# Opening of a hybrid streaming encoder step: token tiles multiplied by norm_pre into buffers of their own

## The chip, the cores and the metric

The kernel runs on one core of a Trainium2 chip. The metric is the device time of one execution in microseconds, and of several executions the median. Times inside an execution come from the hardware profiler; they are counted from the start of the profiled span.

## The reference

One inference step of a one-layer encoder. Its input is 1024 prompt frames of one new stream and 16 frames of each of 8 running streams (128 sample rows in all), 2048 wide, all in float32.

```python
def rms_norm(x, g):
    xf = x.astype(jnp.float32)
    y = xf * lax.rsqrt(jnp.mean(xf * xf, axis=-1, keepdims=True) + EPS)
    return (y * g.astype(jnp.float32)).astype(x.dtype)
...
h = rms_norm(xp, norm_pre[l])
q_sb, k_sb, v_sb, gate_sb, q_r, k_r, v_r, gate_r = project(h, w_in[l], pos_p)
```

`project` is one product with `w_in` (2048 x 8192), whose columns are the queries, keys, values and gates of eight stick-breaking heads and of eight retention heads. Stick-breaking attention over the past keys, chunked retention, a normalisation per head, a gate, an output product with `w_out` and a second normalisation follow; then `x` is added. The sample rows go through the same with cached keys, values and states. What the change touches is only the first line: `h = x * rstd * norm_pre`, row by row.

## The kernel before

The tokens are nine tiles of 128 rows: eight of the prompt and one of the sample rows. Two groups are projected one after the other. Group 0 has prompt tiles 0 to 3 and the sample tile; group 1 has prompt tiles 4 to 7. A projection needs the normalised tokens transposed, with the 2048 features on the partitions, and keeps them in on-chip memory as two arrays: a high part `mh` (ScalarE writes the value rounded to float32r) and a low part `ml` (VectorE subtracts the high part from the value). The helper `split` (lines 129 and 130) makes both, for tokens and for weights (`wh`, `wl`). A float32 product is then three products: wh by mh, wh by ml, wl by mh, in this order (line 227), for each of 16 blocks of features.

The opening, the first 45 us or so, works on the five tiles of group 0. They are called first to fifth here: prompt tiles 0, 1, 2, 3 and the sample tile. For each of them:

- SP's queue loads the tile (`load_x`, line 356, 1 MB, four buffers `xt`). The gain vector `norm_pre` comes broadcast to all partitions as `gpre` in two loads of half the columns, behind the first tile's load (line 380). Further loads on the same queue are four blocks of weights `wr` for the first projection (line 213), the constants, and then the weights of the next projections.
- `stats` takes the mean square: ScalarE squares the tile and sums (line 362, out to `sq`, sum in `ssq`), VectorE computes mean plus epsilon `p0v` (line 137), ScalarE takes the root (line 138), and VectorE does a reciprocal and four small steps of refinement (lines 139 to 143), which end in `p0r`, the reciprocal root.
- For the first four tiles VectorE builds `dg`, a diagonal matrix with `p0r` on it (line 389). For the fifth it multiplies the whole tile by `p0r` in place (line 396).
- The tile is multiplied by `gpre` in place, in eight pieces of 256 columns (line 392). `PRE_POOL` lists the tiles that GpSimd multiplies: second, third and fourth. VectorE multiplies the first and the fifth. As it is in place, a piece can only be written once ScalarE has squared the tile.
- `turn` transposes it on TensorE: four quarters of four 128x128 blocks each, against `dg` (line 372), which scales by the reciprocal root at the same time, or against the identity for the fifth tile (line 370). The profile shows two matmul rows for each block. The results lie in four PSUM buffers `p0t`, one for each quarter, which the `split` of that quarter empties into `mh` and `ml`.

After the second tile TensorE does the first 48 products of the first projection, for the 256 tokens that are there (accumulator of 256 columns); the products for the other 384 tokens come after the fifth tile. After these the projections run one after the other, while a job (`stage_rest`) normalises and stores the tiles of group 1 in between, and the attention, retention and output stages follow.

A scheduler orders the instructions of each engine from the program's text and its own estimates; each engine then runs its list strictly in that order, and waits on semaphores for what it reads, and for buffers that it overwrites. The order on an engine can thus change where the text is changed only nearby. SP, ScalarE and GpSimd also issue transfers from their lists; SP carries the loads of the opening.

Of the kernel before, what the change touches and what calls it, by code (L numbers as in the profile page):

```python
# [9 lines left out]
F32 = mybir.dt.float32  # L10
F32R = mybir.dt.float32r
AF = mybir.ActivationFunctionType
ALU = mybir.AluOpType
# [3 lines left out]
P = 128  # L17
D = 2048
# [6 lines left out]
NT = PT + 1  # L25
SAMPLE = PT
WQ = 4
PRE_POOL = (1, 2, 3)
PRE_DIAG = (0, 1, 2, 3)
PRE_CUT = 8  # L30
PRE_G = 2
# [27 lines left out]
def tile_hybrid_step(  # L59
# [26 lines left out]
    nc = tc.nc  # L86
# [12 lines left out]
    def x_rows(t):  # L99
        return x_prompt[0, t * P : (t + 1) * P, :] if t < PT else xs_flat  # L100
# [27 lines left out]
    def split(hi, lo, src):  # L128
        nc.scalar.activation(hi, src, AF.Copy)  # L129
        nc.vector.tensor_tensor(lo, src, hi.bitcast(F32), ALU.subtract)  # L130

    def inv_rms(pool, ssq, n, name):
        shape = list(ssq.shape)
        v = pool.tile(shape, F32, name=f"{name}v")
        r = pool.tile(shape, F32, name=f"{name}r")
        u = pool.tile(shape, F32, name=f"{name}u")
        nc.vector.tensor_scalar(v, ssq, 1.0 / n, EPS, ALU.mult, ALU.add)
        nc.scalar.activation(r, v, AF.Sqrt)
        nc.vector.reciprocal(r, r)
        nc.vector.tensor_tensor(u, r, r, ALU.mult)  # L140
        nc.vector.tensor_tensor(u, u, v, ALU.mult)
        nc.vector.tensor_scalar(u, u, -0.5, 1.5, ALU.mult, ALU.add)
        nc.vector.tensor_tensor(r, r, u, ALU.mult)
        return r
# [41 lines left out]
    def drain(job):  # L186
        while job is not None and not job.done:
            tick()
# [20 lines left out]
    def load_w(col):  # L209
        hs, ls = [], []  # L210
        for w in range(KT // WQ):
            wr = wp.tile([P, WQ, P], F32, name="wr", tag="wr")
            nc.sync.dma_start(
                wr,
                w_in[0, w * WQ * P : (w + 1) * WQ * P, col : col + P].rearrange("(k p) e -> p k e", p=P),
            )
            wh = wp.tile([P, WQ, P], F32R, name="wh", tag="wh")
            wl = wp.tile([P, WQ, P], F32R, name="wl", tag="wl")
            split(wh, wl, wr)
            yield w, wh, wl  # L220

    def products(mov, acc, pieces, w, wh, wl):
        hi, lo = mov
        for j in range(WQ):
            for n, (lhs, rhs) in enumerate(((wh, hi), (wh, lo), (wl, hi))):
                for a, (o, m) in zip(acc, pieces):
                    last = nc.tensor.matmul(  # L227
                        a[:, :m],
                        lhs[:, j, :],
                        rhs[w][:, j, o : o + m],  # L230
                        start=(w == 0 and j == 0 and n == 0),
                        stop=(w == KT // WQ - 1 and j == WQ - 1 and n == 2),
                    )
                anchor[0] = last
                tick()
        return last

    def acc_banks(g):
        return [accp.tile([P, 512], F32, name=f"acc{i}", tag=f"acc{i}") for i in range(len(g["pieces"]))]
# [60 lines left out]
    with ExitStack() as s1:  # L300
# [39 lines left out]
        def load_rope(gi):  # L340
            n = GROUPS[gi]["n"]
            ropes[:] = [tp.tile([P, n], F32, name=c, tag=c) for c in ("cosT", "sinT")]
            nc.sync.dma_start(ropes[0], c_cos[gi][:, :n])
            nc.sync.dma_start(ropes[1], c_sin[gi][:, :n])
# [3 lines left out]
        with tc.tile_pool(name="p0", bufs=2) as p0, tc.tile_pool(name="p0s", bufs=1) as p0s, tc.tile_pool(  # L348
            name="p0p", bufs=4, space=PSUM
        ) as p0p:  # L350
            warm = p0s.tile([P, 1], F32, name="warm")
            nc.scalar.activation(warm, eps, AF.Sqrt)

            def load_x(t):
                xt = p0.tile([P, D], F32, name="xt", tag="xt", bufs=4)
                nc.sync.dma_start(xt, x_rows(t))
                return xt

            def mean_square(xt):
                ssq = p0.tile([P, 1], F32, name="ssq", tag="ssq")  # L360
                sq = p0s.tile([P, D], F32, name="sq0", tag="sq0")
                nc.scalar.activation(sq, xt, AF.Square, accum_out=ssq)
                return inv_rms(p0, ssq, D, "p0")

            def turn(q, xt, scale=None):
                pt = p0p.tile([P, 4, P], F32, name="p0t", tag="p0t")
                for j in range(4):
                    blk = xt[:, (4 * q + j) * P : (4 * q + j + 1) * P]
                    if scale is None:
                        nc.tensor.transpose(pt[:, j, :], blk, ident)  # L370
                    else:
                        nc.tensor.matmul(pt[:, j, :], blk, scale, start=True, stop=True)
                return pt

            tiles = g0["tiles"]
            loaded = [load_x(tiles[0])]
            gpre = p0s.tile([P, D], F32, name="gpre")
            for c in range(PRE_G):
                cs = slice(c * D // PRE_G, (c + 1) * D // PRE_G)
                nc.sync.dma_start(gpre[:, cs], norm_pre[0, cs].partition_broadcast(P))  # L380
            loaded += [load_x(t) for t in tiles[1:3]]

            def stats(i):
                xt = loaded[i]
                rstd = mean_square(xt)
                dg = None
                if i in PRE_DIAG:
                    dg = p0.tile([P, P], F32, name="dg", tag="dg")
                    nc.vector.tensor_scalar(dg, ident, rstd, None, ALU.mult)
                for c in range(PRE_CUT):  # L390
                    cs = slice(c * D // PRE_CUT, (c + 1) * D // PRE_CUT)
                    (nc.gpsimd if i in PRE_POOL else nc.vector).tensor_tensor(
                        xt[:, cs], xt[:, cs], gpre[:, cs], ALU.mult
                    )
                if dg is None:
                    nc.vector.tensor_scalar(xt, xt, rstd, None, ALU.mult)
                return dg

            scales = [stats(0)]
            for i, t in enumerate(tiles):  # L400
                if i + 1 < len(tiles):
                    scales.append(stats(i + 1))
                cs = slice(i * P, (i + 1) * P)
                for q in range(KT // 4):
                    pt = turn(q, loaded[i], scales[i])
                    split(mov[0][q][:, :, cs], mov[1][q][:, :, cs], pt)
                if i == 1:
                    w4 = list(load_w(col(4, 0)))
                    loaded += [load_x(t) for t in tiles[3:]]
                    acc = acc_banks(g0)  # L410
                    for w in w4:
                        products(mov, acc[:1], g0["pieces"][:1], *w)
            for w in w4:
                last = products(mov, acc[1:], g0["pieces"][1:], *w)

            nc.sync.dma_start(dec, c_dec)
            load_rope(0)
            with nc.allow_non_contiguous_dma(reason="small gains"):
                nc.sync.dma_start(gains[:, 0, :], sb_gain[0].rearrange("(h p) -> p h", p=P))
                nc.sync.dma_start(gains[:, 1, :], ret_gain[0].rearrange("(h p) -> p h", p=P))  # L420

            def stage_rest():
                for i, t in enumerate(GROUPS[1]["tiles"]):
                    hs = p0s.tile([P, KT, P], F32, name="hs", tag="hs")
                    xt = load_x(t)
                    yield 6

                    rstd = mean_square(xt)
                    nc.vector.scalar_tensor_tensor(xt, xt, rstd, gpre, ALU.mult, ALU.mult)
                    yield 12  # L430
                    for q in range(KT // 4):
                        with tc.issue_after(last.ins) if q == 0 else nullcontext():
                            pt = turn(q, xt)
                        nc.scalar.activation(hs[:, 4 * q : 4 * q + 4, :], pt, AF.Copy)
                        yield 3
                    nc.scalar.dma_start(s_h[:, :, i * P : (i + 1) * P], hs)

            job = Job(stage_rest(), D_REST)
            first = ret_inputs(g0, mov, 0, list(zip(acc, g0["pieces"])))
            ret_values(g0, mov, 0)  # L440
            first = *first[:2], pair["r"][:, :, 0, :], dict(rg=gate(project(g0, mov, col(7, 0)), "rg"))
            drain(job)
# [765 lines left out]
```

## Time and profile before

| | us |
|---|---|
| median of 3 runs | 2405.88 |
| lowest and highest | 2405.13, 2412.4 |
| span of the profiled execution, first to last instruction | 2398.4 |
| TensorE busy in the span | 2331.4 (97%) |
| VectorE, ScalarE, GpSimd busy | 1257.5, 919.6, 643.0 |

The profile gives the span of its execution and no other time for it. In the profile PE is TensorE (PEld its weight load), DVE is VectorE, ACT is ScalarE, POOL is GpSimd and SP the engine that issues most transfers. A row of a time line has the start and the length in us, the engine, the line of the kernel, the operation, the tile written and the tiles read, shapes and a count; in brackets stands how long the engine was idle before and what it waited for. Rows with a count over 1 are merged, and instructions of one engine overlap a little in their rows. A row of DMA issues ends with the size in KB and the time from issue to landing.

### The profile page before, as it was taken

To read this page: it belongs to the slowest core of one execution; us is meant where nothing else is said; L and a number is where in the kernel's file an instruction comes from. 1 tells how busy PE (TensorE), PEld (TensorE's weight loads), DVE (VectorE), ACT (ScalarE), POOL (GpSimd) and SP (SyncE) were. 2 spreads that over 40 slices of the span, in tenths; PEclk is the share of its full clock that TensorE was granted. 3 is DMA by queue.
4 is the path that set the end of the run, shared out by engine and by line. 5 is a ranking of instruction groups with operands and counts; after the bars stand their busy time and mean duration, and the time that the engine had idled before them with its cause. 6 is when DMAs were issued, how large, how long until landed. Compare 5 with 4: busy or idle time off the path is not lost.

```text
span 2398.4 us, 40493 instructions
## 1 busy us (share of the span) xinstructions
PE 2331.4 (97%) x14832; PEld 2093.7 (87%) x14832; DVE 1257.5 (52%) x2434; ACT 919.6 (38%) x1933; POOL 643.0 (27%) x1029
## 2 busy tenths in 40 slices
PE   7999999999999999998999999999999999999998
PEld 7998899999999999988878889889898887878787
DVE  7245545445554555445545554554554665564544
ACT  6323333333333333324433434343343454543343
POOL 3144353444344353443202112020221230000000
PEclk9999999999999999999999999999999999999999
DMA  7658879797889879798975565565565666765554
GB/s 244 164 131 209 162 169 196 169 203 166 184 179 194 184 167 194 176 198 198 200 191 151 139 157 149 133 157 146 142 160 139 157 177 181 231 207 176 191 182 132
DMA packets 674890, 418.68 MB, mean 175 GB/s; under 512 B 224513, under 2 KB 619777, under 8 KB 672257
## 3 DMA queue, kind: packets, MB, share of 16 engines
q1 hardware_dynamic: 524272, 285.99, 47.8%
q0 software_dynamic: 32256, 71.36, 13.6%
q10 hardware_dynamic: 118160, 58.74, 9.1%
q8 instruction: 116, 1.90, 0.4%
q14 instruction: 86, 0.70, 0.1%
HBM read 336.24 MB, written 79.69 MB: 173 GB/s over the span
## 4 chain that ended last, share of the span: by engine, by line
PE 87%; DVE 4%; DMA 4%; issue 2%; ACT 1%; POOL 1%; ACTq 0%; DVEq 0%; SPq 0%; POOLq 0%
PE acc L227 45%; PE accn L286 17%; PE a L1029 5%; PE a L1030 5%; PE a L1028 5%; PE pa L616 3%; PE z L586 2%; DMA wr<-w_in 1%; PE zc L659 1%; PE pd L726 1%; DMA mr<-s_h 1%; DVE wl L130 1%; PE pa L770 1%; DVE out L1090 1%; PE rs L752 1%
## 5 line engine op out<-in xcount | busy, mean ns | idle before, releaser
L227 PE MATMUL acc<-mh,wh 128*128 128x256 f32 (+2 forms) x2304 | 664.3, 341 | 6.4 <-ACT wh L129 6.0
L227 PE MATMUL acc<-ml,wh 128*128 128x384 f32 (+2 forms) x2304 | 663.0, 340 | 0.0
L130 DVE TENSOR_TENSOR wl<-wr,wh 128x512 fp32r<-128x512 f32 (+1 forms) x576 | 392.7, 688 | 515.5 <-ACT wh L129 508.3
L227 PE MATMUL acc<-mh,wl 128*128 128x256 f32 (+2 forms) x2304 | 658.9, 339 | 0.6 <-DVE wl L130 0.5
L129 ACT ACTIVATE wh<-wr 128x512 fp32r<-128x512 f32 (+1 forms) x576 | 356.9, 624 | 713.1 <-PE acc L227 243.4
L227 PEld LDWEIGHTS acc<-mh,wh 128*128 128x128 f32 x2304 | 420.2, 189 | 43.3 <-ACT wh L129 7.1
L227 PEld LDWEIGHTS acc<-mh,wl 128*128 128x128 f32 x2304 | 424.4, 189 | 31.4 <-issue 2.1
L227 PEld LDWEIGHTS acc<-ml,wh 128*128 128x128 f32 x2304 | 422.6, 189 | 33.2 <-issue 5.3
L643 POOL DMA_DIRECT2D kc<-cache_sb_k x512 | 332.4, 655 | 369.8 <-DVE kcT L681 207.5
L286 PE MATMUL accn<-whn,mh 128*128 128x256 f32 x1152 | 329.0, 287 | 0.9 <-ACT whn L129 0.8
L286 PE MATMUL accn<-wln,mh 128*128 128x256 f32 x1152 | 326.2, 283 | 0.7 <-DVE wln L130 0.7
L286 PE MATMUL accn<-whn,ml 128*128 128x256 f32 x1152 | 326.0, 283 | 0.0
L286 PEld LDWEIGHTS accn<-whn,mh 128*128 128x128 f32 x1152 | 220.5, 192 | 10.8 <-issue 6.7
L1029 PE MATMUL a<-wl,mh 128*128 128x512 f32 (+1 forms) x576 | 219.7, 381 | 7.8 <-DVE wl L130 7.8
L286 PEld LDWEIGHTS accn<-wln,mh 128*128 128x128 f32 x1152 | 221.2, 192 | 1.7 <-DVE wln L130 0.9
L286 PEld LDWEIGHTS accn<-whn,ml 128*128 128x128 f32 x1152 | 221.2, 192 | 0.0
L1030 PE MATMUL a<-wh,ml 128*128 128x512 f32 (+1 forms) x576 | 218.9, 380 | 0.0
L1028 PE MATMUL a<-wh,mh 128*128 128x512 f32 (+1 forms) x576 | 218.0, 380 | 0.0
L130 DVE TENSOR_TENSOR wln<-wrn,whn 128x512 fp32r<-128x512 f32 x128 | 87.5, 687 | 119.2 <-ACT whn L129 118.5
L129 ACT ACTIVATE whn<-wrn 128x512 fp32r<-128x512 f32 x128 | 80.1, 633 | 152.2 <-PE accn L286 69.8
L1029 PEld LDWEIGHTS a<-wl,mh 128*128 128x128 f32 x576 | 108.3, 188 | 30.5 <-DVE wl L130 9.9
L479 POOL DMA_DIRECT2D be<-s_be x128 | 94.2, 742 | 132.7 <-DMA s_be<-be 114.7
(189 smaller groups left out, 2604.8 us busy)
## 6 DMA issues: line engine op xcount, KB each, us to landing
wr<-w_in SPq DMA_DIRECT2D x384, 256.0 KB, 4.2
wr<-w_out SPq DMA_DIRECT2D x184, 256.0 KB, 3.6
wrn<-w_in SPq DMA_DIRECT2D x128, 256.0 KB, 3.1
kc<-cache_sb_k POOLq DMA_DIRECT2D x512, 64.0 KB, 4.5
vc<-cache_sb_v SPq DMA_DIRECT2D x64, 512.0 KB, 8.6
xt<-x_prompt SPq DMA_DIRECT2D x8, 1024.0 KB, 5.6
xr<-x_prompt SPq DMA_DIRECT2D x8, 1024.0 KB, 6.2
out<-out ACTq DMA_DIRECT2D x12, 512.0 KB, 2.9
```

What stands on the lines that cost most here:

```text
L129: nc.scalar.activation(hi, src, AF.Copy)
L130: nc.vector.tensor_tensor(lo, src, hi.bitcast(F32), ALU.subtract)
L227: last = nc.tensor.matmul(a[:, :m], lhs[:, j, :], rhs[w][:, j, o : o + m], start=(w == 0 and j == 0 and n == 0), stop=(w == KT // WQ - 1 a ...
L286: anchor[0] = nc.tensor.matmul(a, lhs[q][:, jj, ts], rhs[:, j, :], start=(w == 0 and j == 0 and n == 0 and t % 2 == 0), stop=(w == KT // 2 ...
L479: q.dma_start(raw[32 * i : 32 * i + 32, :].rearrange("p (k a) -> p k a", a=32), s[:, :, 32 * i : 32 * i + 32].rearrange("k (j b) a -> b (k ...
L586: nc.tensor.matmul(z[:, :c], q2[a][:, i * P : (i + 1) * P], k2[b][:, s : s + c], start=(m == 0), stop=(m == 2),)
L616: nc.tensor.matmul(po[:, :P], at[:, j, :], vn[:, j, :], start=(j == 0), stop=(j == t))
L643: nc.gpsimd.dma_start(kc[32 * i : 32 * i + 32, :].rearrange("p (k d) -> p k d", d=32), cache_k[0, 2 * c + j, s * 512 : (s + 1) * 512, h, 3 ...
L659: mm = nc.tensor.matmul(z[r, :], qp[:, j, r], ready[2 * j + c // 2][:, c % 2, :], start=(j == 0), stop=(j == 1),)
L1028: nc.tensor.matmul(a[:, :width], hi[q][:, j, ts], wh, start=(k == 0), stop=False)
L1029: nc.tensor.matmul(a[:, :width], hi[q][:, j, ts], wl, start=False, stop=False)
L1030: nc.tensor.matmul(a[:, :width], lo[q][:, j, ts], wh, start=False, stop=(k == KT - 1))
```

## The change

Each of the five tiles is now multiplied by `gpre` into a buffer of its own, `xg` (two buffers), and no longer in place; the turns read `xg`. The multiplication moves from `stats` into a new function `gain`, which is called ahead of `stats`, so it stands in the text ahead of the square. `PRE_POOL` now lists pairs of a tile and the parity of a piece: of the second and of the fifth tile GpSimd multiplies the odd pieces and VectorE the even ones; the third and fourth tile stay with GpSimd, the first with VectorE. The fifth tile's scaling works on `xg`.

```diff
-PRE_POOL = (1, 2, 3)
+PRE_POOL = ((1, 1), (2, 0), (2, 1), (3, 0), (3, 1), (4, 1))
...
                 if i in PRE_DIAG:
                     dg = p0.tile([P, P], F32, name="dg", tag="dg")
                     nc.vector.tensor_scalar(dg, ident, rstd, None, ALU.mult)
-                for c in range(PRE_CUT):
-                    cs = slice(c * D // PRE_CUT, (c + 1) * D // PRE_CUT)
-                    (nc.gpsimd if i in PRE_POOL else nc.vector).tensor_tensor(
-                        xt[:, cs], xt[:, cs], gpre[:, cs], ALU.mult
-                    )
                 if dg is None:
-                    nc.vector.tensor_scalar(xt, xt, rstd, None, ALU.mult)
+                    nc.vector.tensor_scalar(gained[i], gained[i], rstd, None, ALU.mult)
                 return dg

+            gained = {}
+
+            def gain(i):
+                xt = loaded[i]
+                xg = gained[i] = p0.tile([P, D], F32, name="xg", tag="xg", bufs=2)
+                for c in range(PRE_CUT):
+                    cs = slice(c * D // PRE_CUT, (c + 1) * D // PRE_CUT)
+                    pool = (i, c % 2) in PRE_POOL
+                    (nc.gpsimd if pool else nc.vector).tensor_tensor(xg[:, cs], xt[:, cs], gpre[:, cs], ALU.mult)
+
+            gain(0)
             scales = [stats(0)]
             for i, t in enumerate(tiles):
                 if i + 1 < len(tiles):
+                    gain(i + 1)
                     scales.append(stats(i + 1))
                 cs = slice(i * P, (i + 1) * P)
                 for q in range(KT // 4):
-                    pt = turn(q, loaded[i], scales[i])
+                    pt = turn(q, gained[i], scales[i])
                     split(mov[0][q][:, :, cs], mov[1][q][:, :, cs], pt)
```

More of the change, by code (lines that the diff above doesn't have):

```diff
@@ L389, in stats @@
                     nc.vector.tensor_scalar(dg, ident, rstd, None, ALU.mult)
+                if dg is None:
+                    nc.vector.tensor_scalar(gained[i], gained[i], rstd, None, ALU.mult)
+                return dg
+            gained = {}
+            def gain(i):
+                xt = loaded[i]
+                xg = gained[i] = p0.tile([P, D], F32, name="xg", tag="xg", bufs=2)
                 for c in range(PRE_CUT):
                     cs = slice(c * D // PRE_CUT, (c + 1) * D // PRE_CUT)
-                    (nc.gpsimd if i in PRE_POOL else nc.vector).tensor_tensor(
-                        xt[:, cs], xt[:, cs], gpre[:, cs], ALU.mult
-                    )
-                if dg is None:
-                    nc.vector.tensor_scalar(xt, xt, rstd, None, ALU.mult)
-                return dg
+                    pool = (i, c % 2) in PRE_POOL
+                    (nc.gpsimd if pool else nc.vector).tensor_tensor(xg[:, cs], xt[:, cs], gpre[:, cs], ALU.mult)
+            gain(0)
             scales = [stats(0)]
```

## The prediction

> **What bounds the kernel now.** I began with busy shares and slices on the page, then the stretches of the opening, then the chain and the time lines.
>
> ```profile
> PE 2331.4 (97%) x14832; PEld 2093.7 (87%) x14832; DVE 1257.5 (52%) x2434; ACT 919.6 (38%) x1933; POOL 643.0 (27%) x1029
> PE  7999999999999999998999999999999999999998
> ```
> ```profile
> 0.00:45.00 45.00, 29.30 (x202) 28.22 (x203) 32.16 (x81) 28.93 (x46) 19.18 (x30) 0.96 0.84 275
> 45.00:60.00 15.00, 15.00 (x98) 14.98 (x97) 13.91 (x37) 9.88 (x19) 0.00 (x0) 1.00 0.44 150
> 60.00:190.00 130.00, 129.98 (x1008) 127.00 (x1007) 49.21 (x100) 43.87 (x89) 40.98 (x66) 1.00 0.60 154
> ```
> The columns of a stretch are its length, the busy time of TensorE, its weight load, VectorE, ScalarE and GpSimd, the granted clock, the DMA share and GB/s. TensorE is the bound: 97% busy, and gapless from 45 to 190 us (15.00 of 15.00, then 129.98 of 130.00). Only the first slice is weak: of the first 45 us TensorE works 29.30. The change lies wholly there, so its worth is one number: when the unbroken run of products starts. The chain gives the start of that run, the time line of TensorE what comes before it:
>
> ```profile
> 43.46 16.01 PE acc L227 x99
> ```
> ```profile
> 10.63 6.71 PE L372 MATMUL p0t<-dg,xt 128*128 128x128 f32 x32 [10.63 <-DVE dg L389]
> 19.52 5.44 PE L372 MATMUL p0t<-dg,xt 128*128 128x128 f32 x32 [2.19 <-DVE p0v L137]
> 24.72 0.36 PE L227 MATMUL acc<-mh,wh 128*128 128x256 f32 x1
> 25.04 0.28 PE L227 MATMUL acc<-mh,wl 128*128 128x256 f32 x1
> 30.55 3.73 PE L372 MATMUL p0t<-dg,xt 128*128 128x128 f32 x32
> 35.67 3.81 PE L372 MATMUL p0t<-dg,xt 128*128 128x128 f32 x32 [1.38 <-issue]
> 40.43 0.63 PE L370 MATMUL p0t<-ident,xt 128*128 128x128 f32 x4 [0.95 <-DVE xt L396]
> 43.40 0.44 PE L227 MATMUL acc<-ml,wh 128*128 128x384 f32 x1
> ```
> TensorE turns five token tiles (I call them first to fifth): from 10.63, 19.52, 30.55, 35.67 and 40.43, with the first 48 products (128x256) between the second and third. From 43.40 it never stops. The second tile started late:
>
> ```profile
> 11.57 1.91 ACT L362 ACTIVATE sq<-xt 128x2048 f32<-128x2048 f32 x1 [3.32 <-DMA xt<-x_prompt]
> 13.65 11.95 POOL L392 TENSOR_TENSOR xt<-xt,gpre 128x256 f32<-128x256 f32 x16 [12.27 <-ACT sq L362]
> ```
> GpSimd multiplies the second tile only after its square, eight pieces of 11.95/16 = 0.75 us from 13.65 to 19.6.
>
> **The change, part by part.** Counts do not change: 24 multiplies on GpSimd, 16 on VectorE, the same loads. The built programs have the same order on TensorE, GpSimd and SP; only about a hundred instructions of VectorE and ScalarE are reordered.
>
> *First tile.* Now all eight multiplies stand ahead of the reciprocal, four even ahead of the mean (p0v). They need the gain vector, which comes in two loads:
>
> ```profile
> 1.26 0.89 SPq L380 DMA_DIRECT2D gpre<-norm_pre  x2
> gpre<-norm_pre SPq DMA_DIRECT2D x1, 512.0 KB, 6.5
> 1.73 0.42 SPq L380 DMA_DIRECT2D gpre<-norm_pre  x1
> gpre<-norm_pre SPq DMA_DIRECT2D x1, 512.0 KB, 7.2
> 7.86 0.15 DVE L137 TENSOR_SCALAR p0v<-ssq 128x1 f32<-128x1 f32 x1 [6.36 <-ACT sq L362]
> 10.30 0.28 DVE L389 TENSOR_SCALAR dg<-ident,p0r 128x128 f32<-128x128 f32 x1
> 10.49 0.75 DVE L392 TENSOR_TENSOR xt<-xt,gpre 128x256 f32<-128x256 f32 x2
> 28.55 0.17 DVE L139 RECIPROCAL p0r<-p0r 128x1 f32<-128x1 f32 x1 [0.27 <-ACT p0r L138]
> 28.74 0.16 DVE L140 TENSOR_TENSOR p0u<-p0r 128x1 f32<-128x1 f32 x1
> ```
> The halves land at 7.8 and 8.9. Two multiplies in a row take 0.75, so each adds 0.34. Four run from 7.8 to 9.15, p0v then stands at 9.15 instead of 7.86, four more run to 10.55, and only then come the reciprocal and four dependent small steps at 0.19 each: dg at 11.5, done 11.8. Before, those steps were hidden between the multiplies. TensorE starts at 11.85, **1.2 us later**. If the gain vector came a microsecond earlier, 0.2 of it would remain.
>
> *Second tile.* Four pieces each on GpSimd and VectorE, from the landing at 11.5 and without the square. Both engines then read two tiles at once:
>
> ```profile
> 30.97 1.77 DVE L392 TENSOR_TENSOR xt<-xt,gpre 128x256 f32<-128x256 f32 x2
> 45.89 0.63 ACT L129 ACTIVATE wh<-wr 128x512 fp32r<-128x512 f32 x1
> 16.65 1.90 ACT L362 ACTIVATE sq<-xt 128x2048 f32<-128x2048 f32 x1
> 16.60:20.05 3.45, 1.26 (x11) 1.10 (x11) 3.11 (x8) 3.22 (x6) 3.45 (x6) 1.00 1.05 399
> 20.05:23.46 3.41, 3.41 (x19) 3.41 (x18) 2.38 (x5) 1.81 (x5) 3.41 (x5) 0.51 0.98 379
> ```
> Beside GpSimd a piece took 1.77/2 = 0.88 instead of 0.34; four from 11.7 end at 15.2. That is early enough, since the diagonal comes later: it now follows two low parts of the first tile, whose second quarter is turned at 11.85 + 16 x 0.21 + 0.4 = 15.6 (6.71/32 = 0.21 a turn), split by 17.0, and three small steps and dg bring 17.8. The first tile's turns end at 11.85 + 6.7 = 18.5. So the second tile starts at 18.4, 1.1 earlier, without the 2.2 us pause. That pause preceded a stretch at a granted clock of 0.51. Without it I take the 3.73 of the third tile for its 32 turns: end at **22.1** instead of 24.7. Its bounds are 3.73 and 6.7 (the first tile's cold rate). ScalarE is the next limit: the third tile's square (1.90) now precedes the third and fourth high parts of the first tile, which end near 19.2; with 0.6 for each high part of a tile or a weight, the second tile's last high part ends near 22.9. The two new buffers make GpSimd's third tile wait for the first one's turns, 18.5; eight pieces of 0.75 end at 24.5, long before the turn at 30.5. GpSimd's first key load also waits for three token loads of the opening now; it waited already for a store that comes after them.
>
> *What is late next: the first low weight.* In VectorE's built order the first low part of the weights (wl) now stands behind all four low parts of the second tile and behind a small step of the third tile (p0r), where before it ran at 20.12:
>
> ```profile
> 20.12 0.98 DVE L130 TENSOR_TENSOR wl<-wr,wh 128x512 fp32r<-128x512 f32 x1
> 24.93 0.69 DVE L143 TENSOR_TENSOR p0r<-p0r,p0u 128x1 f32<-128x1 f32 x1
> 26.93 1.28 DVE L130 TENSOR_TENSOR wl<-wr,wh 128x512 fp32r<-128x512 f32 x2
> 25.54 0.68 DVE L130 TENSOR_TENSOR ml<-p0t,mh 128x512 fp32r<-128x512 f32 x1
> ```
> The third product needs it. High part at 22.9, low part 0.68, p0r 0.15 to 0.69, wl 0.64 to 0.98: ready between 24.4 and 25.3, or 25.6 if earlier blocked small steps push the low parts back. I take 25.0, near the blocked rows, since GpSimd is busy with the third and fourth tiles from 18.5 on. So the third product starts at 25.0 against 25.04: **the whole gain of the second tile is waited away**, and the next weight load, which reuses that buffer, is issued some 4 us later than at 21.13:
>
> ```profile
> 21.13 3.10 SPq L213 DMA_DIRECT2D wr<-w_in  x1
> 17.41 0.34 SPq L356 DMA_DIRECT2D xt<-x_sample  x1
> 39.02 1.27 DVE L396 TENSOR_SCALAR xt<-xt,p0r 128x2048 f32<-128x2048 f32 x1
> ```
> That costs nothing: the weights are first read at 45.89. The fifth tile's load no longer waits for TensorE's turns of the first (17.41); SP can issue it near 14. It costs nothing and brings nothing, as its square has slack.
>
> *Third to fifth tile.* Products end at 25.0 + 46 x 0.12 = 30.5 (the 48 took (30.55 - 24.72)/48 = 0.12 each). The third tile turns to 34.2, and the fourth no longer waits 1.38: the banks that it needs are freed by the third tile's low parts, which stood behind multiplies (30.97). Now they stand behind the small steps of two tiles, blocked until GpSimd is done near 31, and three rotary steps that wait for the end of the first products; I put the first low part's end at 33.2. It runs from 34.2 to 38.
>
> The fifth tile's buffer is free only when the third tile is turned, 34.3. Four pieces on GpSimd at 0.75 to 0.9 end at 37.3 to 37.9, then the scaling (1.27) to 39.2, then the fourth tile's low parts at 0.64: the fifth starts at 39.8, its last quarter at 41.8, and the run of products at **42.2 instead of 43.40**. With unblocked pieces it is 41.6; with wl at 25.6 and one more blocked piece (0.88) 43.7.
>
> *Sum.* +1.2 at the start, -2.6 by the second tile, back to 0 at the third product, -1.2 at the end: the span 2398.4 becomes 2397.2. The profile gives no time beside the span; the runs' median 2405.88 stands 7.5 above it, so I forecast 2404.7. Bounds of the opening: wl at 24.4 and unblocked pieces, -2.4 (2403.5); the late end, 43.7, +0.3 (2406.2).
>
> **Rivals.**
> *The clock drops in the new pause (slower).* TensorE would now wait from 22.1 to 25.0 for the first low weight. In the row of 16.60 to 20.05 it was busy 1.26 of 3.45, and the next 3.41 ran at 0.51. If the new wait leaves a stretch of 3.4 that empty, 3.41 x 0.5 = 1.7 is lost: -1.2 becomes +0.5, 2406.4. It decides from a pause of about 2.2 up; against it, the 1.38 pause at 34 lost nothing.
> [...]
>
> *The low weight is early (faster).* If GpSimd blocks VectorE nowhere, the lower bounds above hold together: -2.4, 2403.5. Against it, GpSimd is busy from 18.5 to 30 with two tiles, and the rows of VectorE beside it (0.98, 0.69) are the blocked ones.
>
> *The shift is not passed on (no change).* Past 190 us TensorE does wait:
>
> ```profile
> 190.00:240.00 50.00, 44.67 (x299) 41.27 (x298) 24.23 (x42) 17.07 (x37) 20.73 (x37) 1.00 0.86 203
> 202.16 14.15 DMA wr<-w_in x2
> wr<-w_in SPq DMA_DIRECT2D x384, 256.0 KB, 4.2
> ```
> If that wait for weights is set by the transfers alone, it swallows the 1.2: 2405.9. Against it: its issue follows buffers that TensorE frees.
>
> *A second such stall (slower).* Two loads took 14.15 instead of 4.2 there. A shift of phase that makes one more pair collide costs 10 us: 2415. Only a shift beyond the slack of the weight buffers would do it; about 1 us hardly is.
>
> **How the numbers follow.** Forecast 0.38, clock drop 0.30, no shift 0.12, early low weight 0.10, second stall 0.07, unexplained gain 0.03. 0.3% is 7.2 us, about what a measurement of this kernel tells from no change; all but the last two lie within it: 0.03 faster, 0.90 same, 0.07 slower. The forecast alone spans 2403.5 to 2406.2; with the rivals and the spread of the three runs (2405.13 to 2412.4) I take 2401 to 2410.
>
> **What would show it.** Right: first turn near 11.85 behind dg; second tile from 18.4 without a pause; TensorE waiting at its third product for VectorE's wl; the fourth tile without a pause; products unbroken from about 42.2. Wrong: a second tile at the cold rate; wl later than 26, which moves everything after it; a fifth tile held by GpSimd beyond 40; or a span that differs by more than the opening does.

## The result, and the profile after

The changed kernel takes 2409.36 us (median), the kernel before, run beside it, 2404.91. The ratio is 1.0019 with a 95% interval of 1.0013 to 1.0026: some 4.5 us slower, less than the 0.3% that the prediction called no change, but more than this comparison is uncertain. The prediction had 2404.7, a gain of 1.2 against its 2405.88.

The profiled execution of the changed kernel took 2408.77 us with a span of 2407.1. A time is thus 1.7 above its span, and it is 1.7 to 1.8 above it in every run of the whole kernels. So the execution before that I worked from took about 2400.1, and not a time near the median: it was one of the quick ones. Its span and this one differ by 8.7, twice what the medians do; the pair is no measure, the time lines are.

The busy shares of the page after, and TensorE's time line of the opening (start, length, then what ended the pause):

```profile
PE 2336.9 (97%) x14832; PEld 2098.1 (87%) x14832; DVE 1261.4 (52%) x2434; ACT 918.7 (38%) x1933; POOL 644.3 (27%) x1029
```
```profile
12.42 5.88 PE L372 MATMUL p0t<-dg,xg 128*128 128x128 f32 x32 [12.42 <-DVE dg L389]
18.48 3.81 PE L372 MATMUL p0t<-dg,xg 128*128 128x128 f32 x32 [0.18 <-DVE dg L389]
22.04 0.37 PE L227 MATMUL acc<-mh,wh 128*128 128x256 f32 x1
24.59 0.39 PE L227 MATMUL acc<-mh,wl 128*128 128x256 f32 x1 [2.07 <-DVE wl L130]
30.62 7.31 PE L372 MATMUL p0t<-dg,xg 128*128 128x128 f32 x64
40.23 1.71 PE L370 MATMUL p0t<-ident,xg 128*128 128x128 f32 x8 [2.29 <-DVE ml L130]
42.17 1.91 PE L370 MATMUL p0t<-ident,xg 128*128 128x128 f32 x8
43.73 0.56 PE L227 MATMUL acc<-ml,wh 128*128 128x384 f32 x1
```

TensorE is busy 5.5 us longer than in the execution of before (2336.9 against 2331.4) for the same 14832 instructions. The sequence is the forecast one: a late first tile, a second tile at 18.48 without a pause, a wait of the third product for wl, the third and fourth tile in one piece, a fifth tile at 40.23. Two things differ: the first turn is later than 11.85, and the fifth tile runs at half rate (1.91 us for eight rows, where an execution of the kernel before, shown below, took 1.03). The unbroken products start at 43.73, not at 42.2. That is only 0.3 after the 43.40 of the profile before, so this pair does not show where the loss of 4.5 comes from; the experiments had to. VectorE, and GpSimd beside it:

```profile
11.53 0.83 DVE L389 TENSOR_SCALAR dg<-ident,p0r 128x128 f32<-128x128 f32 x1
18.04 0.29 DVE L389 TENSOR_SCALAR dg<-ident,p0r 128x128 f32<-128x128 f32 x1
23.15 0.68 DVE L130 TENSOR_TENSOR ml<-p0t,mh 128x512 fp32r<-128x512 f32 x1
23.86 0.68 DVE L130 TENSOR_TENSOR wl<-wr,wh 128x512 fp32r<-128x512 f32 x1
```
```profile
11.55 3.15 POOL L402 TENSOR_TENSOR xg<-xt,gpre 128x256 f32<-128x256 f32 x4 [10.18 <-DMA xt<-x_prompt]
18.38 12.98 POOL L402 TENSOR_TENSOR xg<-xt,gpre 128x256 f32<-128x256 f32 x16 [3.67 <-DVE dg L389]
```

The first diagonal `dg` starts at 11.53, as forecast, but lasts 0.83 instead of 0.28: GpSimd begins its share of the second tile at 11.55. The first low weight `wl` stands behind the second tile's last low part, as the built order said.

The granted clock explains the fifth tile. Stretches of 3.41 us, cut where the clock changes; the columns are TensorE, its weight load, VectorE, ScalarE and GpSimd busy, the granted clock, the DMA share and GB/s:

```profile
20.15:23.56 3.41, 2.38 (x22) 2.17 (x20) 3.35 (x9) 3.26 (x8) 3.41 (x6) 1.00 1.01 373
23.56:26.97 3.41, 2.21 (x16) 2.01 (x17) 3.41 (x6) 3.38 (x4) 3.41 (x5) 1.00 0.63 93
37.22:40.63 3.41, 1.12 (x11) 0.93 (x9) 3.30 (x5) 1.61 (x4) 0.68 (x1) 1.00 0.55 159
40.63:44.04 3.41, 3.41 (x17) 3.00 (x16) 2.68 (x6) 2.66 (x3) 0.00 (x0) 0.50 0.51 216
```

The pause at the third product happened to be cut in two by a boundary; with 2.38 and 2.21 us of work the two stretches were followed by full speed. The pause before the fifth tile left 1.12 in one stretch, and the next ran at 0.50.

### The profile page after: what moved, and what is told of

Read it like the earlier page. It is cut to its first block, busy times and chain, and to the rows that moved or that the text cites. A ratio compares the mean times of both kernels' runs of the same rounds, so it can differ in the third digit from the quotient of the medians.

```text
span 2407.1 us, 40493 instructions
## 1 busy us (share of the span) xinstructions
PE 2336.9 (97%) x14832; PEld 2098.1 (87%) x14832; DVE 1261.4 (52%) x2434; ACT 918.7 (38%) x1933; POOL 644.3 (27%) x1029
## 4 chain that ended last, share of the span: by engine, by line
PE 84%; DMA 6%; DVE 4%; issue 2%; ACT 2%; SPq 1%; POOL 0%; DVEq 0%; ACTq 0%; POOLq 0%
PE acc L227 45%; PE accn L286 17%; PE a L1036 4%; PE a L1037 4%; PE a L1035 4%; DMA mr<-s_y 3%; PE pa L623 3%; PE z L593 2%; DMA wr<-w_in 2%; PE zc L666 1%; PE pd L733 1%; DMA mr<-s_h 1%; DVE wl L130 1%; PE pa L777 1%; DVE out L1097 1%
```

## Experiments

Three explanations of the 4.5 us stood against each other; the expectations, put down before each run, call them theories A, B and D, in this order, and theory C is that past the opening executions differ by chance alone. *Fixed stretches*: half-speed stretches come at fixed times, and the change only moves work into them. *After the opening*: the shift makes some wait for weights longer. *The opening itself*: its new pauses, with the half-speed stretches that follow them. Within the last there were three suspects: the first tile's place ahead of its statistics, the sharing, and the two buffers.

### The kernel before again, and the changed kernel again

No edit; each kernel is run once more, to see how much one execution says.

> The kernel before, a second time and with a second profile. Theory A (clock windows): the 3.41 us windows that set TensorE's clock sit at the same times after the start in every execution, so the half-speed windows are those of the first profile again: near 20, 269 (two), 1116, 1143 and 1211 us, and the opening's run of products starts at 43.4. Theory C (chance): past the opening the half-speed windows and waits differ from execution to execution as much as between the first profiles of before and after, so this profile differs from the first by several us with no edit at all. Time: 2404.9 in both, ratio 1.000.

Measured: 2403.17, ratio 0.9999 (0.9988 to 1.0011).

> The changed kernel, a second time and with a second profile. Theory A: half-speed windows near 41, 222, 235, 273 (two), 1095, 1133, 1150, 1222 and 2140 us again, TensorE 0.5 us late at 45 us and some 3.5 us late at 240. Theory B (something of the change itself acts after the opening): the same waits are longer again, at 222 and 235 above all. Theory C: the opening is the same (0.5 late), the rest is scattered anew. Time in all three near 2409.4, ratio 1.002.

Measured: 2407.94, ratio 1.0018 (1.0006 to 1.0029). The loss repeats, so it was no chance of the first comparison. The first of these traces ruled out fixed stretches: by the clock's records the half-speed stretch in the opening of the kernel before lies at another time than in the profile shown ahead (none at 20 us, one at 35, where the fourth tile turns at half rate):

```profile
34.20 5.44 PE L372 MATMUL p0t<-dg,xt 128*128 128x128 f32 x32 [2.06 <-issue]
```

The changed kernel's repeated trace has two in the opening, at 26 and 43 us, where the profile above has one. Its products start unbroken at 46.54, those of the kernel before at 41.94.

### The kernel before, its opening made later

```diff
                 if dg is None:
+                    nc.vector.tensor_scalar(xt, xt, 1.0, None, ALU.mult)
                     nc.vector.tensor_scalar(xt, xt, rstd, None, ALU.mult)
```

> The kernel before with one more pass of VectorE over the fifth tile (times 1.0, 1.2 us) ahead of its scaling: the run of products starts about 0.8 us late, at 44.2, and nothing else of the change is there. Theory A: a small shift against the fixed windows and the transfers costs more than itself: +3 to +5, 2408 to 2410, with half-speed windows near 222 and 235 as in the changed kernel. Theory B and theory C: +0.8 and no more, 2405.7.

Measured: 2405.59, ratio 1.0008 (0.9997 to 1.0020). The extra pass moved the second half of the fifth tile's turns from 41.09, in the repetition of the kernel before, to 41.92. The result agrees with that being passed on and with no change; this run settles nothing by itself.

### The changed kernel with three buffers for the products

```diff
-                xt = p0.tile([P, D], F32, name="xt", tag="xt", bufs=4)
+                xt = p0.tile([P, D], F32, name="xt", tag="xt", bufs=3)
...
-                xg = gained[i] = p0.tile([P, D], F32, name="xg", tag="xg", bufs=2)
+                xg = gained[i] = p0.tile([P, D], F32, name="xg", tag="xg", bufs=3)
```

> The changed kernel with three buffers xg and three xt: the fifth tile's multiplication waits for the turns of the second tile, not of the third. TensorE's pause ahead of the fifth tile (37.7 to 40.2) and the half-speed window at 41 to 44 go, and the run of products starts near 40.5 instead of 44.1, 3 us ahead of the kernel before. Theory B: 3.5 us less than the changed kernel, 2405.9. Theory C: 3 us less than before, 2402. Theory A: which later windows run at half speed changes again; the time lies anywhere from 2400 to 2408 and does not follow the opening.

Measured: 2406.48, ratio 1.0014 (1.0002 to 1.0026). TensorE's time line of this run:

```profile
26.68 0.39 PE L227 MATMUL acc<-mh,wl 128*128 128x256 f32 x1 [3.20 <-DVE wl L130]
41.37 1.25 PE L370 MATMUL p0t<-ident,xg 128*128 128x128 f32 x8 [0.22 <-DVE ml L130]
```

The fifth tile's pause went from 2.29 to 0.22, but the products start at 43.78, not near the expected 40.5, since the wait for wl is 3.20 and a half-speed stretch follows it. The loss is 3.0 us by the medians; its interval, 0.5 to 6.2 us, does not tell whether the third buffer took any of it away.

### Both kernels cut behind the opening

A spread of 10 us between executions hides where a loss of 4.5 arises. Both kernels were therefore cut behind group 0's first projections, where their spans are some 116 to 121 us; attention, retention and the output stages are left out.

```diff
             drain(job)
+        return
```

> The kernel before cut off after its opening (group 0's first projections and the staging of group 1 are there, some 105 us; attention, retention and output are left out). Its median is the reference for the next two runs; the order of the opening is that of the whole kernel. Theory A fell with the second profiles: the slow windows lie at other times in each execution. Theory D (the opening with its pauses, over all positions of the windows, holds the loss) and theory B (half or more of it arises after the opening) differ in the next run. Here both expect some 105 to 115 us with a spread of 1 to 3 us between executions.

Measured: 118.38 us (118.30 to 120.03, five runs), mean clock 0.985 or 0.986 in each. Rows of TensorE's and one row of VectorE's time line:

```profile
10.49 5.70 PE L372 MATMUL p0t<-dg,xt 128*128 128x128 f32 x32 [10.49 <-DVE dg L389]
18.80 3.81 PE L372 MATMUL p0t<-dg,xt 128*128 128x128 f32 x32 [2.61 <-DVE p0v L137]
22.68 0.28 PE L227 MATMUL acc<-mh,wl 128*128 128x256 f32 x1
34.14 5.44 PE L372 MATMUL p0t<-dg,xt 128*128 128x128 f32 x32 [2.06 <-issue]
41.04 1.03 PE L370 MATMUL p0t<-ident,xt 128*128 128x128 f32 x8
41.88 0.44 PE L227 MATMUL acc<-ml,wh 128*128 128x384 f32 x1
19.39 0.98 DVE L130 TENSOR_TENSOR wl<-wr,wh 128x512 fp32r<-128x512 f32 x1
```

> The changed kernel cut off at the same place. Theory D: its median is 3.5 to 5 us above the cut kernel before, the whole of the +4.4 measured for the full kernels, because two pauses of more than 2 us (third product, fifth tile) can each cost a slow window. Theory B: 0 to 2 us above, as the sum of the prediction with one slow window has it (+0.5), and the rest must come after 105 us.

Measured: 122.45 us (120.56 to 124.31, seven runs). The time lines of the changed kernel, cut:

```profile
12.71 5.17 PE L372 MATMUL p0t<-dg,xg 128*128 128x128 f32 x32 [12.71 <-DVE dg L389]
18.92 3.81 PE L372 MATMUL p0t<-dg,xg 128*128 128x128 f32 x32 [1.04 <-DVE p0v L137]
26.16 0.58 PE L227 MATMUL acc<-mh,wl 128*128 128x256 f32 x1 [3.19 <-DVE wl L130]
33.11 7.31 PE L372 MATMUL p0t<-dg,xg 128*128 128x128 f32 x64
42.71 1.89 PE L370 MATMUL p0t<-ident,xg 128*128 128x128 f32 x8 [2.30 <-DVE ml L130]
46.37 0.42 PE L227 MATMUL acc<-ml,wh 128*128 128x384 f32 x1
17.94 0.83 DVE L389 TENSOR_SCALAR dg<-ident,p0r 128x128 f32<-128x128 f32 x1
24.81 1.29 DVE L130 TENSOR_TENSOR wl<-wr,wh 128x512 fp32r<-128x512 f32 x1
20.58 0.62 ACT L129 ACTIVATE wh<-wr 128x512 fp32r<-128x512 f32 x1
```

122.45 - 118.38 = 4.07: nearly the whole loss of the full kernels is there, without attention, retention and output. In the two profiled executions the products start unbroken at 46.37 against 41.88, 4.5 later, and the spans differ by the same (120.9 and 116.4). Nothing is left that asks for "after the opening"; the interval of the full kernels (3.1 to 6.3 us) cannot exclude a small rest.

The rows also show the way. The first turn is 2.2 later, but the second tile only 0.1, since it waits 1.04 and no longer 2.61. Then the kernel before goes on: its wl was made at 19.39, between the low parts, and the third product runs at 22.68. In the changed kernel wl comes at 24.81, lasts 1.29 beside GpSimd, and the third product runs at 26.16, 3.5 later. ScalarE's high part of that weight, which wl needs, is also later, but it is done at 21.20 (20.58 + 0.62) and wl starts 3.6 after it: it is VectorE's order that holds wl. What follows the pause runs at half speed:

```profile
22.37:25.78 3.41, 0.60 (x6) 0.39 (x4) 3.39 (x7) 3.41 (x6) 3.41 (x6) 1.00 0.71 139
25.78:29.20 3.42, 3.04 (x14) 3.04 (x15) 3.42 (x5) 2.63 (x4) 3.42 (x4) 0.50 0.44 125
```

This pause does not make the loss alone. With it the third tile starts at 33.11, and it and the fourth run in one piece to 40.4. The kernel before waits 2.06 ahead of its fourth tile and turns it at half rate, to 39.6 (34.14 + 5.44). So the changed kernel is only 0.8 behind when the fourth tile ends; the rest of the 4.5 arises at its fifth tile, with a pause of 2.30 and a second half-speed stretch.

By the mean clock the seven runs fall into three groups: 0.986 (120.56, 121.00, 121.00), 0.972 (122.45, 122.73) and 0.958 (124.09, 124.31). One stretch of 3.41 at half speed is 1.7 of about 119, or 0.014, so by this estimate these are one, two and three such stretches, and each further one costs about 1.6 to 1.7 us. The kernel before had one in every run, but its times at the same clock fall into two groups: 118.30, 118.30 and 118.38, and 119.84 and 120.03, of which no trace was kept. Where its one stretch falls may be the difference: with the stretch on the second tile the first profile's products started at 43.40, with the stretch on the fourth tile those of the two repetitions at 41.94 and 41.88. At one stretch each the change costs 1.9 us by the means (120.85 against 118.97), or 2.5 against the median of the kernel before; this is the pauses. The rest of the 4.07 is the one more stretch of the median run.

### The first tile's multiplies put back behind its statistics

Everything else stays: buffers of its own, sharing, the other tiles ahead of their squares.

```diff
-            gain(0)
+            gained[0] = None
             scales = [stats(0)]
+            gain(0)
```

> The changed kernel cut off at the same place, with the first tile's multiplication put back behind its statistics; its buffer, and everything of the other tiles, stay as changed. VectorE's list then has the small steps of the first tile between the multiplies, and the first low part of the weights ahead of the second tile's low parts, as in the kernel before. If the first tile's place is what costs (both theories for the opening): first turn at 10.6, no pause at the third product, 3 to 5 us less than the cut changed kernel, and 0 to 2 less than the cut kernel before. If the sharing or the buffers cost: no better than 1 us below the cut changed kernel.

Measured, cut: 118.75 us (118.53 to 118.92, four runs), 3.7 less than the cut change, as expected, but 0.4 more than the cut kernel before and not less.

```profile
11.13 5.97 PE L372 MATMUL p0t<-dg,xg 128*128 128x128 f32 x32 [11.13 <-DVE dg L389]
19.51 3.81 PE L372 MATMUL p0t<-dg,xg 128*128 128x128 f32 x32 [2.41 <-DVE p0v L137]
23.39 0.28 PE L227 MATMUL acc<-mh,wl 128*128 128x256 f32 x1
38.81 1.60 PE L370 MATMUL p0t<-ident,xg 128*128 128x128 f32 x8 [2.21 <-DVE p0v L137]
42.18 0.67 PE L227 MATMUL acc<-ml,wh 128*128 128x384 f32 x1
20.22 0.98 DVE L130 TENSOR_TENSOR wl<-wr,wh 128x512 fp32r<-128x512 f32 x1
```

> The whole changed kernel with the first tile's multiplication put back behind its statistics. Theory D: it follows the cut kernels, 0 to 2 us under the kernel before (2402 to 2404) and some 4 to 6 under the changed one. Theory B: what arises after the opening stays, 2 to 4 us over the kernel before.

Measured, whole kernel: 2404.24, ratio 0.9998 (0.9987 to 1.0009).

This one edit removes the loss, cut and whole, as far as the intervals show. It does so in the medians only: the one profiled execution of the whole kernel has half-speed stretches at 20 and at 40 us and starts its products at 44.12, no earlier than the changed kernel's 43.73. The cut one still has the pause of 2.21 ahead of the fifth tile, with a half-speed stretch behind it, and yet starts its products only 0.3 after the kernel before, which has its own pause and stretch at the fourth tile. So the fifth tile's pause costs next to nothing where it takes the place of that one; where it comes on top of the pause at the third product, as in the changed kernel, it costs the most.

The edit changes two things at once: `dg` comes earlier, and the scheduler, whose order follows from the text, puts wl back ahead of the second tile's low parts (20.22). That the second is what pays is my reading of the time lines (in the cut pair the second tile is 0.1 late and the third product 3.5); I did not move wl alone.

### One part alone, cut

The multiplies ahead of the statistics, into buffers of their own, without sharing; then the sharing alone, in place and behind the squares.

```diff
-PRE_POOL = ((1, 1), (2, 0), (2, 1), (3, 0), (3, 1), (4, 1))
+PRE_POOL = ((1, 0), (1, 1), (2, 0), (2, 1), (3, 0), (3, 1))
```

> The changed kernel cut behind the opening as before (attention, retention and output are left out), with the buffers of its own and the multiplies ahead of the statistics, but without the sharing: GpSimd multiplies the second tile whole and none of the fifth, as in the kernel before. VectorE's order keeps the first weight's low part (wl) behind all low parts of the second tile. Theory of the first tile's place (the multiplies ahead of the mean and the reciprocal, and the order that goes with them): the loss stays, between 120.5 (one half-speed window) and 124 (three), against 118.4 of the cut before and 122.45 of the cut change; the third product waits 2 us or more for wl. Rival, that the sharing is needed for the loss, since it puts GpSimd beside VectorE at the second and the fifth tile: 119.2 or less.

Measured: 122.38 us (120.67 to 122.93, four runs).

```profile
26.31 0.58 PE L227 MATMUL acc<-mh,wl 128*128 128x256 f32 x1 [3.19 <-DVE wl L130]
```

The loss is complete without any sharing, with the same pause. (This section's and the next one's cut kernels ran on a second chip; there the whole kernel before took 2403.54 us, against 2404.00 on the first, but no cut kernel before was run there.) Then the other part, as a diff against the kernel before:

```diff
-PRE_POOL = (1, 2, 3)
+PRE_POOL = ((1, 1), (2, 0), (2, 1), (3, 0), (3, 1), (4, 1))
...
-                    (nc.gpsimd if i in PRE_POOL else nc.vector).tensor_tensor(
+                    (nc.gpsimd if (i, c % 2) in PRE_POOL else nc.vector).tensor_tensor(
```

> The kernel before, cut behind the opening as before, with the sharing alone: in place, behind the square, the odd pieces of the second and the fifth tile on GpSimd and the even ones on VectorE. VectorE's order keeps wl ahead of the second tile's low parts. Theory of the first tile's place: no loss, 118.4 within 1.0. Rival, that the sharing costs (VectorE's pieces blocked beside GpSimd, the fifth tile late): 119.5 or more.

Measured: 121.98 us (120.85 to 122.67, four runs). My expectation fell: sharing alone costs 3.6.

```profile
10.46 5.24 PE L372 MATMUL p0t<-dg,xt 128*128 128x128 f32 x32 [10.46 <-DVE dg L389]
19.74 5.44 PE L372 MATMUL p0t<-dg,xt 128*128 128x128 f32 x32 [4.03 <-issue]
36.64 1.43 PE L372 MATMUL p0t<-dg,xt 128*128 128x128 f32 x8 [2.13 <-POOL xt L392]
44.48 0.44 PE L227 MATMUL acc<-ml,wh 128*128 128x384 f32 x1
13.65 1.29 DVE L392 TENSOR_TENSOR xt<-xt,gpre 128x256 f32<-128x256 f32 x2
17.28 0.68 DVE L130 TENSOR_TENSOR ml<-p0t,mh 128x512 fp32r<-128x512 f32 x1
19.36 0.27 DVE L389 TENSOR_SCALAR dg<-ident,p0r 128x128 f32<-128x128 f32 x1
```

Here VectorE's four pieces of the second tile wait for the square until 13.65 and hold the first tile's low parts (first one at 17.28) and the second diagonal (19.36) behind them. TensorE waits 4.03 and then turns the second tile at half speed (5.44 instead of 3.81); the fourth tile waits 2.13 for GpSimd. With buffers of its own the pieces start when the tile has landed, and the run with the first tile put back, which shares too, lost next to nothing (0.4 cut, no difference whole). So the parts do not add: either alone costs about 4, both together also 4, and both without the first tile's move next to nothing. At one half-speed stretch (mean clock 0.985 or 0.986) this holds too: 118.30 to 120.03 before, 120.56 to 121.00 changed, 118.53 to 118.92 with the first tile put back, and one run each of 120.67 without sharing and 121.48 with sharing alone. In the runs with sharing alone the clock does not order the times: 120.85 came at 0.971.

### A version with both repairs

The first tile put back, and three buffers for the products.

> The cut kernel with the first tile's multiplies back behind its statistics, and three buffers for the products instead of two (three instead of four for the loaded tiles): the fifth tile's multiply can run as soon as the second tile is turned, so the pause of 2.2 us ahead of the fifth tile should go. If that pause has the price that the time lines give it, the cut kernel takes 117 (between 116 and 117.8) against 118.75 with two buffers. If the fifth tile then waits as long for something else: 118.4 or more.

Measured, cut: 117.91 us (117.79 to 118.00, four runs), 0.8 less than with two buffers and 0.5 less than the kernel before.

```profile
33.87 5.44 PE L372 MATMUL p0t<-dg,xg 128*128 128x128 f32 x32 [1.93 <-DVE p0u L142]
41.32 0.44 PE L227 MATMUL acc<-ml,wh 128*128 128x384 f32 x1
```

This lies just outside the expected 116 to 117.8. The fifth tile follows the fourth at once, but now the fourth waits 1.93. Its diagonal is ready at 31.6; by the order of the rows it waits for the third tile's first low part, which ends at 33.72 and frees a PSUM buffer. That is late since the fifth tile's multiplies stand between the small steps of the fourth tile's statistics on VectorE, and ScalarE's high parts behind a root that waits for these. About half of the hoped-for 1.75 us is missing.

> The same edit in the whole kernel, as a candidate to beat both. If what the opening gains is passed on to the end: 2402.5 against some 2404 of the kernel before (ratio 0.9993, between 0.9988 and 0.9999). If the loading of the weights swallows it: 2404, no difference.

Measured, whole kernel: 2402.74, ratio 0.9998 (0.9989 to 1.0007). If the 0.5 is there, the whole kernel cannot tell it from nothing.

## Why the prediction was wrong

Forecast was a gain of 1.2 us; measured is a loss of 4.5 (3.1 to 6.3 by the interval). The median, 2409.36, still lies in the forecast range of 2401 to 2410, but that range was made wide by the spread and the rivals, and the direction was wrong.

- *The level.* "the runs' median 2405.88 stands 7.5 above it" took the difference of one quick execution from the median for a constant. It is 1.7. This moved the forecast's level, not its difference.
- *First tile, +1.2.* Right in direction, too small: dg was put at 0.28 "done 11.8", and it lasts 0.83 beside the GpSimd work that the change itself starts at that moment (11.55). The first turn came at 12.42 to 12.71 in the changed kernel.
- *Second tile, -2.6.* Start and end came out (18.48, and the first product at 22.04), the start in part by luck: the first turn was 0.6 later than forecast, and the first tile's turns took 5.88 and not 6.7. But the gain was not the change's. The 24.7 of the kernel before belonged to an execution whose half-speed stretch fell on the second tile. In the cut one it fell at 35 us, the second tile took 3.81 and the third product ran at 22.68. The bound of 6.7, "the first tile's cold rate", was not reached; the granted clock of the profile before shows 1.00 from 10.60 to 16.60, so no record here shows a low clock as what slowed those turns.
- *Third product, "25.0 against 25.04".* This is the step that failed: the sum put the shift at this point at 0. Both numbers are mis-sized: 22.68 stands for the kernel before when the clock does not drop on the second tile (22.75 in the repetition of the whole kernel), and 26.16 for the changed kernel when a small step and wl last longer beside GpSimd (0.77 and 1.29 in the cut one; 24.59 in the profile above, with 0.19 and 0.68). Not "the whole gain of the second tile is waited away": no gain was there, and the third product is 3.5 us late. With the half-speed stretch behind it this pause is the start of the loss. The bound of 25.3 to 25.6 was exceeded in four of five traces with this order (26.16 to 26.68).
- *Third and fourth tile.* Right: 64 rows in one piece, 7.31. The pause and the half-speed stretch that the kernel before has there are gone, so the fourth tile ends only 0.8 late in the cut pair.
- *Fifth tile, 39.8.* 40.23 in the profile: the pause was seen, its consequence for the clock was put at nothing. It left 1.12 us of work in a stretch, and the next ran at half speed; so the products started at 43.73 instead of 42.2 although the third product, at 24.59, was earlier than forecast.
- *The rival.* "The clock drops in the new pause" is what happens, with chance 0.30 and a price of 1.7. The price (1.6 to 1.7 by the groups of the cut runs) and the order of events were right, and it can strike twice: at the third product and at the fifth tile. The kernel before has such a stretch in its opening too, so that only the additional ones count. The rival's own sum, +0.5, still fell 4 us short, because it stood on the same 25.0 against 25.04.
- *Passed on or not.* Cut, a late opening arrives whole (4.5 later products, 4.5 longer span; in the other four cut traces the two shifts agree within 0.4). The rival in which a later wait swallows the shift is not borne out by the full kernels, where 4.07 in the cut kernels stands beside 4.5 at the end.

## What to carry to other kernels

Before a pause in one trace is counted as a gain, look at a second execution of the unchanged kernel: what the clock did to this one is not what the change removes. When work moves ahead in an in-order queue, find the consumer that the scheduler has put behind it, here a low weight behind four low parts; by the time lines it, and not the moved work, starts the loss. A pause has no fixed price: here one pause with its half-speed stretch took the place of another for nothing, and the second one on top cost the most. Sharing elementwise work between two engines gained nothing by itself in any run here; it did no harm only where the pieces could start as soon as the tile had landed, and with sharing alone, behind the square, the low parts and a diagonal stood behind them.

## What the hardware did that I had not expected

*The half-speed stretches.* In the openings they last 3.41 us. The two of the cut changed kernel begin at 25.78 and 42.85, five such lengths apart; the one of the profile above, at 40.63, lies 4.35 lengths behind 25.78, so the phase differs from execution to execution. A stretch with 1.12 or 0.60 us of TensorE work was followed by half speed, one with 2.21 was not. In between these runs show no bound: of two stretches with nearly the same work the first (1.47), from the cut kernel with the first tile put back, was followed by full speed, and the second (1.48), from the one with three buffers as well, by half speed:

```profile
15.63:19.05 3.42, 1.47 (x13) 1.28 (x12) 2.78 (x7) 2.81 (x4) 1.87 (x3) 1.00 1.11 388
19.05:22.46 3.41, 2.95 (x26) 2.98 (x27) 3.29 (x9) 2.68 (x7) 3.41 (x6) 1.00 0.99 394
```
```profile
31.01:34.42 3.41, 1.48 (x14) 1.32 (x13) 3.06 (x11) 2.64 (x6) 0.46 (x1) 1.00 1.04 380
34.42:37.84 3.42, 3.42 (x19) 3.42 (x18) 3.35 (x6) 2.40 (x4) 0.00 (x0) 0.50 0.62 256
```

A pause of 2.30 us that lay within one stretch was followed by half speed (ahead of 42.71 above; the next stretch ran at 0.50), and one of 2.07, which a boundary cut in two, by full speed (ahead of 24.59 in the profile above).

*VectorE beside GpSimd.* While GpSimd's pieces ran, a diagonal took up to 0.84 (the first one of the cut changed kernel) instead of the 0.28 ahead of them, but also 0.27 (at 24.09 in the cut kernel before), and a low weight up to 1.29, but also 0.68 (in the profile above), while the low parts of tokens, which read PSUM, stayed at 0.67 to 0.69. The rows show these lengths; what makes the difference was not shown. In these two traces the time line tips with it: in the profile above GpSimd begins its third tile at 18.38, just after the second diagonal (0.29 from 18.04); in the cut one it begins at 17.97, and the diagonal takes 0.83.
